# Two score components side by side in a two-bank PSUM tile, and a values product with the queries moving, in a two-layer hybrid encoder

## The chip, the cores and the metric

The kernel runs on one core of a Trainium2 chip. The core has five engines, each with its own queue of instructions: TensorE (PE, with its weight loads shown as PEld), VectorE (DVE), ScalarE (ACT), GpSimd (POOL) and SyncE (SP), which issues the DMAs here. They share an on-chip memory of 128 partitions (SBUF); TensorE writes its results into PSUM, which has eight banks of 512 float32 per partition. The metric is the device time of one execution in microseconds, the median of several runs; lower is better.

## The reference

Two layers of a bidirectional encoder on 512 tokens of width 1024, in float32. Each layer projects the normed input to two groups of heads, puts their outputs through one output projection, and ends in a gated feed-forward with a short convolution. The change concerns the scores of both groups and the values and norm of group B:

```python
def one_block(qi):                      # group B: differential attention
    s = jnp.einsum('bqhcd,bkhcd->bhcqk', qi, k) * scale      # c: two components of 64
    p = jax.nn.softmax(s, axis=-1)
    w = p[:, :, 0] - lam * p[:, :, 1]
    return jnp.einsum('bhqk,bkhd->bqhd', w, v)               # v: 128 wide
...
ya = windowed_gqa_sink(qa, ka, va, sink[l])                  # group A: 8 heads of 64, window of 3 blocks
yb = diff_attention(qb, kb, vb, lam)                         # group B: 4 heads
yb = rmsnorm(yb, subln[l]) * (1.0 - lambda_init)
y = jnp.concatenate([ya, yb], axis=-1)
x = x + y @ w_out[l]
h = rmsnorm(x, g_ffn[l])
gate, val = jnp.split(h @ w_up[l], 2, axis=-1)
x = x + (silu(dwconv(gate)) * val) @ w_down[l]
```

## The kernel before

**Numbers.** Every product is made with float32r operands split into a high and a low part, as three matmuls (`mm3`, lines 193 to 196: high by high, high by low, low by high). `split_out` (line 245) makes the two parts: ScalarE rounds, VectorE subtracts.

**Stages.** The residual lies transposed in SBUF, as eight tiles of 128 features by 512 tokens. Weights come from DRAM in units of up to 512 KB, issued by SP, and are split by ScalarE (line 181) and VectorE or POOL (line 182), three units ahead of their use. In each layer come the input projection (`project`, 24 matmuls with 256 moving columns per block of 128 tokens), the attention of group A and group B, the output projection (`out_pass`, `out_tail`, `out_last`), the norm, and the feed-forward (`up` and `dn`).

**Order.** `weave` (line 121) mixes two tracks of program order by the costs that each step yields: `attend()`, with a total of ATT = 92, and the track of projections for group B and of most of the output projection, with a total of 98.6. A step that yields a function waits until that holds. `out_last(1)`, the second half of the last pass of the output projection, runs behind the weave. From the program order the framework builds a list per engine with its own model of time, in which an instruction that is ready may go ahead of an earlier one that isn't; a tile is taken from its pool when its first writer is placed, and given back behind its last reader.

**PSUM.** Eight banks: two of tag `mm` (projections), four single banks of tag `at` (scores and transposes), one `acc` (sums over many products), one `tq` (small transposes).

**Group A** (`a_scores`, `a_values`). For each of 2 x 4 pairs of head group and query block, twice: two heads' scores, each with 64 rows of contraction on its own half of the partitions, in two banks. Six matmuls, with 256 or 384 key columns, alternate the two (line 412). The masked maximum, the softmax and a division follow; then each key block is transposed (line 457), split and multiplied with the values.

**Group B** (`b_scores`, `b_values`, `b_norm`). For each half (two heads), query block `qb` and head `j`: six matmuls of 512 key columns for components 0 and 1 (line 502), two maxima (line 505), two exps that also sum (line 509), the difference of the weights (line 517). Two units later (LAG = 2): four transposes of the weights (line 529), the split, and 12 matmuls with the transposed weights stationary and 128 value columns moving (lines 538 to 541), so that queries lie on partitions. Per query block and half `b_norm` copies, squares, sums along the row (line 556), takes the root on POOL (`rsqrt`, line 243), scales (line 562), transposes back (line 566) and splits (lines 575 and 576).

Of the kernel before, what the change touches and what calls it, by code (L numbers as in the profile page):

```python
# [34 lines left out]
YP = 3  # L35
# [8 lines left out]
def kernel(  # L44
# [32 lines left out]
    def prob(name):  # L77
        return sb.tile([P, S], F32R, tag="prob", bufs=6, name=name)

    def tmp(name, n=S):  # L80
        return sb.tile([P, n], F32, tag="tmp", bufs=7, name=name)
# [3 lines left out]

    def yp(name):
        return sb.tile([P, CW], F32, tag="yp", bufs=YP, name=name)

# [9 lines left out]
    def at(name):  # L98
        return ps.tile([P, S], F32, tag="at", bufs=4, name=name)
# [9 lines left out]
    def wide(name):  # L109
        cyc["i"] += 1  # L110
        return (mm, at, at)[cyc["i"] % 3](name)
# [155 lines left out]
    for l in range(depth):  # L267
        lam_init = 0.8 - 0.6 * math.exp(-0.3 * l)
# [98 lines left out]
        # group A keys and values, then queries  # L367
# [10 lines left out]
        run(project("akv", akv_done, at))  # L378
# [9 lines left out]
        banks = iter((mm, mm, at, at, at, at, mm, mm))  # L388
# [10 lines left out]
        def a_scores(ip, qb):  # L399
# [7 lines left out]
            for i in range(2):  # L407
                sc = [at(f"sc_{nm}_{i}_{g}") for g in range(2)]
# [36 lines left out]
        def a_values(ip, qb):  # L445
# [6 lines left out]
            for b in range(nkb):  # L452
                tr = at(f"pt_{nm}_{b}")
                for g in range(2):
                    for i in range(2):
                        o = (2 * g + i) * P
                        nc.tensor.transpose(tr[:, o:o + P], so[2 * i + g][:, b * P:(b + 1) * P], ident)
                ph = prob(f"ph_{nm}_{b}")
                pl = prob(f"pl_{nm}_{b}")
                split_out(ph, pl, tr)  # L460
                pb.append((ph, pl))
                yield 0.5
# [25 lines left out]
        def b_scores(half, qb, j):  # L488
            h = 2 * half + j
            if j == 0:  # L490
                b_st[half, qb] = small(f"bl{l}_{half}_{qb}", 4)
            lsum = b_st[half, qb]
# [5 lines left out]
            sc = [at(f"sc_{nm}_{c}") for c in range(2)]  # L498
# [5 lines left out]
            for c in range(2):  # L504
                nc.vector.tensor_reduce(out=mx[:, c:c + 1], in_=sc[c], axis=AX, op=ALU.max)  # L505
            nc.vector.scalar_tensor_tensor(out=mx, in0=mx, scalar=-1.0, in1=rq, op0=ALU.mult, op1=ALU.mult)  # L506
            for c in range(2):
                e.append(tmp(f"e_{nm}_{c}"))
                nc.scalar.activation(e[c], sc[c], AF.Exp, bias=mx[:, c:c + 1], scale=rq[:, c:c + 1],  # L509
                                     accum_out=lsum[:, 2 * j + c:2 * j + c + 1])  # L510
                yield 0.65
            rl = small(f"rl_{nm}", 1)
            nc.vector.reciprocal(rl, lsum[:, 2 * j + 1:2 * j + 2])
            al = small(f"al_{nm}", 1)
            nc.vector.tensor_scalar(out=al, in0=lsum[:, 2 * j:2 * j + 1], scalar1=rl, scalar2=nlam,
# [4 lines left out]
        def b_values(half, qb, j):  # L520
            h = 2 * half + j
            nm = f"b{l}_{h}_{qb}"
            if j == 0:
                b_st[half, qb, "acc"] = accum(f"yb{l}_{half}_{qb}")
            yb = b_st[half, qb, "acc"]
            w = b_st.pop((half, qb, j))
            tr = (mm if half and j else at)(f"wt_{nm}")
            for b in range(NT):
                nc.tensor.transpose(tr[:, b * P:(b + 1) * P], w[:, b * P:(b + 1) * P], ident)
            wh, wl = prob(f"wth_{nm}"), prob(f"wtl_{nm}")  # L530
            split_out(wh, wl, tr)
            yield 0.5
            for first in (True, False):
                for b in range(NT):
                    vh, vl = (v[:, b % 2 * CW + j * P:b % 2 * CW + j * P + P] for v in vb[half, b // 2])
                    o = slice(b * P, (b + 1) * P)
                    if first:
                        nc.tensor.matmul(yb[:, j * P:(j + 1) * P], lhsT=wh[:, o], rhs=vh, start=b == 0, stop=False)
                        nc.tensor.matmul(yb[:, j * P:(j + 1) * P], lhsT=wh[:, o], rhs=vl, start=False, stop=False)
                    else:  # L540
                        nc.tensor.matmul(yb[:, j * P:(j + 1) * P], lhsT=wl[:, o], rhs=vh, start=False, stop=b == NT - 1)
            yield 1.3

        def b_norm(half, qb):
            nm = f"yb{l}_{half}_{qb}"
            yb = b_st.pop((half, qb, "acc"))[:, :2 * P]
            lsum = b_st.pop((half, qb)).rearrange("p (t c) -> p t c", c=2)[:, :, 0]
            le = small(f"le_{nm}", 2)
            nc.vector.scalar_tensor_tensor(out=le, in0=lsum, scalar=EPS / (1.0 - lam_init) ** 2, in1=lsum,
                                           op0=ALU.mult, op1=ALU.mult)  # L550
            y = yp(f"y_{nm}")
            nc.scalar.copy(y, yb)
            sq = yp(f"sq_{nm}")
            nc.scalar.activation(sq, y, AF.Square)
            ss = small(f"ss_{nm}", 2)
            nc.vector.tensor_reduce(out=ss, in_=sq.rearrange("p (t d) -> p t d", d=P), axis=AX, op=ALU.add)
            g2 = (1.0 - lam_init) ** 2
            nc.vector.scalar_tensor_tensor(out=ss, in0=ss, scalar=1.0 / (P * g2), in1=le, op0=ALU.mult, op1=ALU.add)
            rr = small(f"rr_{nm}", 2)
            rsqrt(rr, ss)  # L560
# [19 lines left out]
        def attend():  # L580
# [4 lines left out]
            def values():  # L585
# [5 lines left out]
                else:  # L591
                    yield from b_values(kind, qb, j)
                    while norms:
                        yield from norms.pop(0)
# [201 lines left out]
```

## Time and profile before

| what | value |
|---|---|
| median of 3 runs | 1309.32 us (1308.12 to 1310.32) |
| span of the profiled execution | 1302.4 us |
| mean granted TensorE clock | 0.991 |
| instructions in the profile | 17571 |
| attention, layer 0, from the first scores of A to the last values of B | about 55 to 285 us |
| attention, layer 1 | about 697 to 923 us |
| DMA | 102.96 MB, mean 79 GB/s |

The profile is of one execution; its span runs from the first to the last instruction of the program and is 6.9 us shorter than the median of the runs. "Busy" time of TensorE runs to the modelled end of each matmul and overlaps with the next one, so the distance between two starts tells better what a matmul takes.

### The profile page before, as it was taken

How to read it: one execution, taken by the hardware profiler on the slowest of the kernel's cores; microseconds unless marked ns; L12 is line 12 of the kernel's file. 1: busy time of each engine (PE TensorE's matmuls, PEld its weight loads, DVE VectorE, ACT ScalarE, POOL GpSimd, SP SyncE). 2: the span in 40 equal slices, each digit the busy share in tenths (PEclk: the TensorE clock that was granted, in tenths of full speed). 3: DMA queues.
4: the chain of work that ended last, by engine and by line, in shares of the span. 5: the costliest groups of instructions: out<-in, count | busy, mean ns of one | idle time of the engine just before them, and what ended most of it. 6: DMA issues, size and time to landing. Idle time of an engine off the chain costs nothing. (4 is left out here: it accounts for less than half of the span.)

```text
span 1302.4 us, 17571 instructions
## 1 busy us (share of the span) xinstructions
PE 1270.6 (98%) x6744; PEld 1056.6 (81%) x6744; DVE 772.9 (59%) x1425; ACT 557.5 (43%) x1027; POOL 385.4 (30%) x446
## 2 busy tenths in 40 slices
PE   6999899999999999999999999999899999999998
PEld 6988788687888888888899878877788888888887
DVE  7678787767655324554466786767765543355532
ACT  4566555435433223333455656544443332233321
POOL 6847376114211000110156654741411110011100
PEclk8999999999999999999999999999999999999999
DMA  5211112113332233332331211111133322433232
GB/s 181 91 33 49 58 33 65 33 33 97 98 97 85 85 106 97 98 97 79 100 98 66 65 33 33 56 59 33 33 113 97 97 81 94 117 98 98 79 106 90
DMA packets 32628, 102.96 MB, mean 79 GB/s; under 512 B 3616, under 2 KB 4000, under 8 KB 32544
## 3 DMA queue, kind: packets, MB, share of 16 engines
q1 hardware_dynamic: 32544, 101.84, 25.6%
q8 instruction: 53, 0.87, 0.3%
q14 instruction: 31, 0.25, 0.1%
HBM read 99.73 MB, written 2.10 MB: 78 GB/s over the span
## 5 line engine op out<-in xcount | busy, mean ns | idle before, releaser
L181 ACT CAST wh<-wr 128x1024 fp32r<-128x1024 f32 (+3 forms) x210 | 197.7, 944 | 400.1 <-PE up L195 192.0
L195 PE MATMUL up<-nf_l,wh 128*128 128x512 f32 x704 | 275.3, 391 | 2.3 <-DVE nf_l L213 1.9
L196 PE MATMUL up<-nf_h,wl 128*128 128x512 f32 x704 | 274.5, 390 | 1.2 <-DVE wl L182 0.9
L194 PE MATMUL up<-nf_h,wh 128*128 128x512 f32 x704 | 272.9, 390 | 0.0
L182 DVE TENSOR_TENSOR wl<-wr,wh 128x1024 fp32r<-128x1024 f32 (+3 forms) x174 | 193.3, 1114 | 112.2 <-ACT wh L181 111.8
L702 POOL TENSOR_TENSOR cv<-cv,rb 128x512 f32<-128x512 f32 x44 | 57.8, 1316 | 521.5 <-ACT cv L701 521.5
L195 PEld LDWEIGHTS up<-nf_l,wh 128*128 128x128 f32 x704 | 132.1, 188 | 33.6 <-DVE nf_l L213 6.6
L196 PEld LDWEIGHTS up<-nf_h,wl 128*128 128x128 f32 x704 | 132.1, 188 | 29.7 <-DVE wl L182 2.9
L194 PEld LDWEIGHTS up<-nf_h,wh 128*128 128x128 f32 x704 | 132.2, 188 | 27.6
L195 PE MATMUL dn<-act,wh 128*128 128x512 f32 x352 | 138.5, 394 | 0.0
L196 PE MATMUL dn<-act,wl 128*128 128x512 f32 x352 | 138.4, 394 | 0.0
L194 PE MATMUL dn<-act,wh 128*128 128x512 f32 x352 | 137.9, 393 | 0.0
L182 POOL TENSOR_TENSOR wl<-wr,wh 128x1024 fp32r<-128x1024 f32 x36 | 87.1, 2421 | 89.4 <-ACT wh L181 89.4
L695 DVE TENSOR_TENSOR gp<-up,rb 128x512 f32<-128x512 f32 x44 | 30.3, 693 | 103.4 <-PE up L196 101.8
L703 DVE TENSOR_TENSOR cv<-cv,up 128x512 f32<-128x512 f32 x44 | 30.2, 687 | 82.6 <-POOL cv L702 73.0
L194 PEld LDWEIGHTS dn<-act,wh 128*128 128x128 f32 x352 | 66.0, 188 | 16.0
L195 PEld LDWEIGHTS dn<-act,wh 128*128 128x128 f32 x352 | 66.0, 187 | 15.7
L196 PEld LDWEIGHTS dn<-act,wl 128*128 128x128 f32 x352 | 66.0, 188 | 15.4
L716 DVE TENSOR_TENSOR x<-x,dn 128x512 f32<-128x512 f32 x32 | 22.0, 689 | 78.4 <-PE dn L196 78.4
L509 ACT ACTIVATE e_b<-sc_b,mx_b,rqb 128x512 f32<-128x512 f32 x64 | 49.2, 774 | 38.6 <-DVE mx_b L506 38.6
L701 ACT ACTIVATE cv<-cv 128x512 f32<-128x512 f32 x44 | 27.8, 632 | 76.4 <-DVE cv L700 76.3
L505 DVE TENSOR_REDUCE mx_b<-sc_b 128x1 f32<-128x512 f32 x64 | 42.0, 681 | 0.2
(211 smaller groups left out, 2713.7 us busy)
## 6 DMA issues: line engine op xcount, KB each, us to landing
wr<-w_up SPq DMA_DIRECT2D x88, 512.0 KB, 3.6
wr<-w_in SPq DMA_DIRECT2D x36, 512.0 KB, 3.7
wr<-w_down SPq DMA_DIRECT2D x32, 384.0 KB, 3.1
wr<-w_down SPq DMA_DIRECT2D x32, 320.0 KB, 2.9
wr<-w_out SPq DMA_DIRECT2D x16, 512.0 KB, 3.6
x<-xT SPq DMA_DIRECT2D x8, 256.0 KB, 5.3
outT<-x SPq DMA_DIRECT2D x8, 256.0 KB, 2.0
rows<-row_par SPq DMA_DIRECT2D x2, 260.0 KB, 5.0
```

The costliest lines, as they stand in the source:

```text
L181: nc.scalar.copy(hi[:, o], raw[:, o])
L182: eng.tensor_tensor(out=lo[:, o], in0=raw[:, o], in1=hi[:, o], op=ALU.subtract)
L194: nc.tensor.matmul(acc, lhsT=a[0], rhs=b[0], start=start, stop=False)
L195: nc.tensor.matmul(acc, lhsT=a[0], rhs=b[1], start=False, stop=False)
L196: nc.tensor.matmul(acc, lhsT=a[1], rhs=b[0], start=False, stop=stop)
L505: nc.vector.tensor_reduce(out=mx[:, c:c + 1], in_=sc[c], axis=AX, op=ALU.max)
L509: nc.scalar.activation(e[c], sc[c], AF.Exp, bias=mx[:, c:c + 1], scale=rq[:, c:c + 1], accum_out=lsum[:, 2 * j + c:2 * j + c + 1])
L695: nc.vector.tensor_tensor(out=g[:, 1:S + 1], in0=acc[0], in1=rb, op=ALU.mult)
L701: nc.scalar.activation(cv, cv, AF.Silu)
L702: nc.gpsimd.tensor_tensor(out=cv, in0=cv, in1=rb, op=ALU.mult)
L703: nc.vector.tensor_tensor(out=cv, in0=cv, in1=acc[1], op=ALU.mult)
L716: nc.vector.tensor_tensor(out=x_sb[d], in0=x_sb[d], in1=acc, op=ALU.add)
```

## The change

Scores get a tile of two banks, `at2` (two such tiles in place of four single banks); group A's two heads and group B's two components each take one whole tile. `both` gives its two halves, `wide2` and `halves` hand out pairs of banks to the stages that took single ones. Group A's transposes take one half of such a tile, the `tq` bank or an `mm` bank, by key block. The two maxima of group B become one instruction over both banks.

In group B the order of units becomes half, pair of query blocks `qp`, head, block in the pair. The transposes and the split (`b_weights`) write 128 of 256 columns per key block; after the second block `b_values` multiplies with the values stationary and 256 queries moving, so that the 128 value features lie on partitions. `b_norm` runs once per pair: the square's sum over partitions is a product with `ones`, the root comes back to all partitions through a product with `ident`, and no transposes are needed at its end. ATT and LAG keep their values. Pool sizes change: `prob` from six single to four double tiles, `tmp` from 7 to 8, the rotary tables from four tags of one to one tag of three, and `yp` goes.

```diff
-    def at(name):
-        return ps.tile([P, S], F32, tag="at", bufs=4, name=name)
+    def at2(name):
+        return ps.tile([P, 2, S], F32, tag="at", bufs=2, name=name)
...
-    def wide(name):
+    def wide2(name):
         cyc["i"] += 1
-        return (mm, at, at)[cyc["i"] % 3](name)
+        if cyc["i"] % 3 == 0:
+            return mm(f"{name}a"), mm(f"{name}b")
+        t = at2(name)
+        return t[:, 0], t[:, 1]
+
+    def halves(pick):
+        have = []
+
+        def alloc(name):
+            if not have:
+                have.extend(pick(name))
+            return have.pop(0)
+        return alloc
+
+    def both(name):
+        t = at2(name)
+        return t[:, 0], t[:, 1]
...
-                tabs[i] = sb.tile([P, 2, NT, HD], F32, tag=f"tab{i}", bufs=1, name=f"tab{l}_{i}")
+                tabs[i] = sb.tile([P, 2, NT, HD], F32, tag="tab", bufs=3, name=f"tab{l}_{i}")
...
-        run(project("akv", akv_done, at))
+        run(project("akv", akv_done, halves(both)))
...
-                sc = [at(f"sc_{nm}_{i}_{g}") for g in range(2)]
+                sc = both(f"sc_{nm}_{i}")
...
-                tr = at(f"pt_{nm}_{b}")
+                tr = mm(f"pt_{nm}_{b}") if b == 2 else both(f"pt_{nm}_{b}")[0] if b == 0 else tq(f"pt_{nm}_{b}")
...
-            sc = [at(f"sc_{nm}_{c}") for c in range(2)]
+            sc2 = at2(f"sc_{nm}")
+            sc = (sc2[:, 0], sc2[:, 1])
             for i, (u, v) in enumerate(((0, 0), (0, 1), (1, 0))):
                 for c in range(2):
                     rs = slice(c * HD, (c + 1) * HD)
                     nc.tensor.matmul(sc[c], lhsT=q[u][rs, j, qb * P:(qb + 1) * P], rhs=k[v][rs, j, :],
                                      start=i == 0, stop=i == 2)
-            for c in range(2):
-                nc.vector.tensor_reduce(out=mx[:, c:c + 1], in_=sc[c], axis=AX, op=ALU.max)
+            nc.vector.tensor_reduce(out=mx, in_=sc2, axis=AX, op=ALU.max)
...
+        def b_weights(half, qb, j):
...
+            tr = (mm(f"wt_b{l}_{h}_{qb}") if half and j else both(f"wt_b{l}_{h}_{qb}")[0])
             for b in range(NT):
                 nc.tensor.transpose(tr[:, b * P:(b + 1) * P], w[:, b * P:(b + 1) * P], ident)
-            wh, wl = prob(f"wth_{nm}"), prob(f"wtl_{nm}")
-            split_out(wh, wl, tr)
+            o = slice(qb % 2 * P, qb % 2 * P + P)
+            split_out(wt[0][:, :, o], wt[1][:, :, o], tr.rearrange("p (b q) -> p b q", b=NT))
             yield 0.5
-            for first in (True, False):
-                for b in range(NT):
...
-            yield 1.3
+        def b_values(half, qp, j):
...
+            for b in range(NT):
+                vh, vl = (v[:, b % 2 * CW + j * P:b % 2 * CW + j * P + P] for v in vb[half, b // 2])
+                mm3(yb, (vh, vl), (wt[0][:, b], wt[1][:, b]), b == 0, b == NT - 1)
+                if b % 2:
+                    yield 0.7
+
+        def b_norm(half, qp):
...
+            nc.scalar.activation(y, yb, AF.Copy, scale=cols[:, l, c3:c3 + 1])
+            sq = tmp(f"sq_{nm}")
+            nc.scalar.activation(sq, yb, AF.Square)
...
+            yield 0.2
+            ss = tq(f"ss_{nm}")
+            for i in range(4):
+                nc.tensor.matmul(ss[:, i:i + 1], lhsT=sq[:, i * P:(i + 1) * P], rhs=ones, start=True, stop=True)
+            rr = small(f"rr_{nm}", 4)
+            nc.vector.scalar_tensor_tensor(out=rr, in0=ss[:, :4], scalar=1.0 / (P * (1.0 - lam_init) ** 2), in1=le,
+                                           op0=ALU.mult, op1=ALU.add)
+            rsqrt(rr, rr)
+            yield 0.5
+            rt = tq(f"rt_{nm}")
+            for i in range(4):
+                nc.tensor.matmul(rt[:, i * P:(i + 1) * P], lhsT=rr[:, i:i + 1].broadcast_to([P, P]), rhs=ident,
+                                 start=True, stop=True)
+            nc.vector.tensor_tensor(out=y, in0=y, in1=rt, op=ALU.mult)
...
+            split_out(yh, yl, y.rearrange("p (j q) -> p j q", j=2))
+            b_st["yb", half, qp] = True
+            yield 0.5
...
-            seq += [(half, qb, j) for half in range(2) for qb in range(NT) for j in range(2)]
+            seq += [(half, 2 * qp + i, j) for half in range(2) for qp in range(2) for j in range(2) for i in range(2)]
...
+                yield from b_weights(kind, qb, j)
+                if norms:
+                    yield from norms.pop(0)
+                if qb % 2:
+                    yield from b_values(kind, qb // 2, j)
+                    if j:
+                        g = b_norm(kind, qb // 2)
+                        yield next(g)
+                        norms.append(g)
...
-        run(out_last(1, w_last, wide))
+        run(out_last(1, w_last, halves(wide2)))
...
-                acc = []
+                acc = wide2(f"up{l}_{f}")
                 for j in range(2):
                     w = next_unit()
-                    a = wide(f"up{l}_{f}_{j}")
                     for k in range(NK):
-                        mm3(a, (w[0][:, k, :], w[1][:, k, :]), (h.hi[k], h.lo[k]), k == 0, k == NK - 1)
-                    acc.append(a)
+                        mm3(acc[j], (w[0][:, k, :], w[1][:, k, :]), (h.hi[k], h.lo[k]), k == 0, k == NK - 1)
...
+            wide = halves(wide2)
```

More of the change, by code (lines that the diff above doesn't have):

```diff
@@ L34 @@
 RP = 7
-YP = 3
 SMP = 12
@@ L387 @@
         qk = {}
-        banks = iter((mm, mm, at, at, at, at, mm, mm))
+        pairs_at = halves(both)
+        banks = iter((mm, mm, pairs_at, pairs_at, pairs_at, pairs_at, mm, mm))
         run(proj_a(0, lambda name: next(banks)(name)))
@@ L550, in b_norm @@
                                            op0=ALU.mult, op1=ALU.mult)
[L551 to L558, printed above, removed]
@@ L590, in values @@
                         b_st["ya"] = True
[L591 to L594, printed above, removed]
-                    if j == 1:
-                        norms.append(b_norm(kind, qb))
-                        yield next(norms[0])
+                    return
+                yield from b_weights(kind, qb, j)
[7 more added lines that the diff above has]
+                        norms.append(g)
             for kind, qb, j in seq:
```

81 lines of the change are left out of this document (30 added, 51 removed).

## The prediction

> **What bounds the kernel now.** I read the engine table of the page first, then the busy time of the four attention stretches (two per layer), then what TensorE waits for.
>
> ```profile
> PE 1270.6 (98%) x6744; PEld 1056.6 (81%) x6744; DVE 772.9 (59%) x1425; ACT 557.5 (43%) x1027; POOL 385.4 (30%) x446
> ```
>
> ```profile
> 55.00:150.00 95.00, 93.45 (x644) 80.21 (x645) 74.87 (x209) 57.86 (x147) 55.70 (x53) 0.98 0.15 47
> 150.00:285.00 135.00, 129.28 (x775) 102.94 (x774) 100.83 (x222) 67.70 (x153) 61.48 (x62) 1.00 0.16 48
> 697.00:790.00 93.00, 90.78 (x620) 77.23 (x616) 71.03 (x207) 55.16 (x140) 47.07 (x45) 0.98 0.16 46
> 790.00:923.00 133.00, 130.01 (x798) 106.41 (x798) 94.52 (x218) 69.06 (x156) 59.41 (x51) 0.99 0.16 48
> ```
>
> Columns of these four rows: stretch, its length, busy PE, PEld, DVE, ACT, POOL, then granted clock. The four stretches are 456 us long; TensorE is busy for 443.5 of them, VectorE for 341.3 (75%).
>
> ```profile
> PE pj_akv L194 <- ACT wh L181: 6.2, 1, 6.2
> ...
> PE tr_yb L566 <- DVE y_yb L562: 2.3, 2, 1.1
> PE yb L541 <- DVE wtl_b L247: 1.9, 2, 1.2
> PE up L195 <- DVE nf_l L213: 1.9, 2, 1.0
> ...
> PE na_ss L233 <- DVE na_sum L227: 0.2, 1, 0.2
> ```
>
> These are the first, the last and three of the sixteen rows of what TensorE waited for; all sixteen sum to 26.8 us, and those of attention to about 13.5. So **TensorE's own work sets the time**, in the order in which its queue holds it, and an edit is worth what it takes from TensorE. "Busy" says little of that work, as matmuls overlap in the pipeline; I price by the distance from one start to the next.
>
> **Scores.** Both components of a head contract over 64 rows, one on partitions 0 to 63, the other on 64 to 127. The first fence has two rows of the group view (behind the bar: busy us as a union, mean ns of one), the next three the order of time (start, length, count).
>
> ```profile
> L502 PE MATMUL sc_b<-bkh,bqh 64*128 64x512 f32 x64 | 27.9, 490 | 0.0
> L412 PE MATMUL sc_a<-ka,qal 64*128 64x256 f32 (+1 forms) x64 | 16.5, 318 | 0.0
> ```
>
> ```profile
> 227.76 0.41 PE L566 MATMUL tr_yb<-ident,y_yb 128*128 128x128 f32 x2
> 228.10 0.50 PE L502 MATMUL sc_b<-bkh,bqh 64*128 64x512 f32 x1
> ...
> 228.99 0.66 PE L529 MATMUL wt_b<-ident,e_b 128*128 128x128 f32 x4
> ```
>
> ```profile
> 882.65 0.50 PE L502 MATMUL sc_b<-bkh,bqh 64*128 64x512 f32 x2
> ...
> 883.54 0.50 PE L194 MATMUL wo<-yh,wh 128*128 128x512 f32 x1
> ```
>
> ```profile
> 102.64 0.50 PE L412 MATMUL sc_a<-ka,qah 64*128 64x256 f32 x4
> ...
> 103.19 0.38 PE L194 MATMUL pj_bk<-wh,na_h 128*128 128x256 f32 x1
> ```
>
> ```profile
> 122.24 0.28 PE L194 MATMUL pj_bk<-wh,na_h 128*128 128x256 f32 x1
> 122.36 0.28 PE L195 MATMUL pj_bk<-wl,na_h 128*128 128x256 f32 x1
> 122.57 0.62 PE L412 MATMUL sc_a<-ka,qah 64*128 64x384 f32 x4
> ...
> 123.30 0.38 PE L196 MATMUL pj_bk<-wh,na_l 128*128 128x256 f32 x1
> ```
>
> At 228.10 one component's three matmuls stand alone and take 0.89 us until the next work. At 882.65 both components' six (rows of x2: pairs with one start) take 0.89 us too. So **a pair costs what one costs**, if its two halves stand next to each other. How many do? In the row of L502, 64 times 490 ns is 31.4 us, the union is 27.9; the missing 3.5 us is 7 overlapping pairs of 32, so 25 heads run apart. L412's row in the same way: 64 x 318 ns = 20.4, less 16.5, is 3.9 us or 12 pairs, so 20 of 32 apart. Before the change each component had its own bank, and the queue took the first as soon as one bank was free. Afterwards one allocation gives both banks, so all six become ready together and their program order alternates the components.
>
> A run that is saved saves its entry as well: before 122.57 the distance is 0.21 where two projections are 0.12 apart, so 0.09. Group B: 25 x (0.89 + 0.09) = **-24.5 us**. Group A: six take 0.73 us at 384 columns and 0.55 at 256 (rows 122.57 and 102.64), half of the blocks each, so 20 x (0.64 + 0.09) = **-14.6**. Bounds: nothing, if the queue still puts other work between the components, and -39.1; the rows with x2 and x4 show that what is ready together stays together, so I take it whole.
>
> **Values product turned round.**
>
> ```profile
> 272.03 0.31 PE L538 MATMUL yb<-vb,wth_b 128*128 128x128 f32 x1
> ...
> 272.96 0.61 PE L541 MATMUL yb<-vb,wtl_b 128*128 128x128 f32 x4
> 273.40 0.45 PE L649 MATMUL wo<-yh_b,wh 128*128 128x256 f32 x2
> ```
>
> Twelve matmuls with 128 moving columns take 272.03 to 273.40, 1.37 us or 0.114 each; with 256 columns the distance is 0.12 (122.24 to 122.36). Before: 32 units of 12, 43.8 us. After: 16 units of 12 at 0.12, 23.0 us. **-20.8**. The transposes of the weights (L529) stay 128 in number, and their split keeps its size.
>
> [...]
>
> **Norm over partitions.** The nearest rows are the same forms in the layer norm: four one-column products (8 passes) and four broadcasts against ident (8 passes), from the chain view.
>
> ```profile
> 948.89 0.79 PE nf_ss L233 x8
> 956.19 0.89 PE rps L673 x8
> ```
>
> Eight norms at 0.79 + 0.89, with two entries of 0.09, add 14.9 us. Sixteen pairs of transposes (L566) go, 0.34 us each from 227.76 to 228.10: -5.4. Net **+9.5**.
>
> **Sum on TensorE**: -24.5 - 14.6 - 20.8 + 9.5 = -50.4 us.
>
> **The end of each attention.**
>
> ```profile
> 282.75 0.40 PE L649 MATMUL wo<-yl_b,wh 128*128 128x256 f32 x2
> 284.28 0.41 PE L566 MATMUL tr_yb<-ident,y_yb 128*128 128x128 f32 x2 [1.13 <-DVE y_yb L562]
> 285.25 0.50 PE L649 MATMUL wo<-yh_b,wh 128*128 128x256 f32 x2 [0.56 <-ACT yh_b L575]
> 285.60:288.80 3.20, 3.20 (x21) 3.20 (x20) 0.11 (x1) 0.00 (x0) 0.00 (x0) 0.63 0.02 5
> ```
>
> The last norm is bare: from 282.75 + 0.24 to 285.25 TensorE does only two transposes (0.24), so 2.0 us are lost, and the clock then reads 0.63 for 3.2 us. The new chain is longer: two ACT passes, ss, a sum, rsqrt on POOL, broadcast, product, cast; with 0.79 and 0.89 for the two matmul steps and 0.685 for the product on VectorE (rows above and below), and five more steps taken as of that order, some 6 to 7 us, an estimate. But the costs that attend() yields fall: group A's stay 39.0, group B's go from 16 x 3.1 + 8 x 0.35 = 52.4 to 16 x 1.8 + 8 x 1.4 + 4 x 1.2 = 44.8. ATT stays 92, so attend() ends when 91% of the other track's 98.6 is out, and about 9 us of output projection are left over to cover the chain. I take both gaps as gone, -4.0, and 0.5 us per layer of the slow clock (1.2 us by the row, but the VectorE chain behind it, the wait of up on nf_l, is late next and keeps most): **-5**.
>
> **Off the path.**
>
> ```profile
> L505 DVE TENSOR_REDUCE mx_b<-sc_b 128x1 f32<-128x512 f32 x64 | 42.0, 681 | 0.2
> L562 DVE TENSOR_TENSOR y_yb<-y_yb,rr_yb 128x256 f32<-128x256 f32 x16 | 9.9, 618 | 2.7 <-POOL rr_yb L243 2.4
> L247 DVE TENSOR_TENSOR act<-cv,act 128x512 fp32r<-128x512 f32 x44 | 30.2, 685 | 1.4 <-ACT act L246 1.4
> ```
>
> VectorE's 64 maxima become 32 of twice the length (between 0.68 and 1.36 us each; I take 1.2, near the upper end, as the length doubles: 42.0 to 38.4). The norm's 16 products of 256 columns become 8 of 512 at 0.685, 9.9 to 5.5, its other steps also halve in number, and one reduction goes. All of that is hidden behind TensorE and worth nothing by itself; with at least 8 us gone, VectorE has at most 333 us in a stretch of some 401, 83% where it was 75%. The new scale and square on ACT read 512 columns where they read 256, half as often: ACT is far from its bound (249.8 us of 456). The fourth rotary table now waits on POOL for one of three buffers, until group A's keys are done; its first reader, bk0, stands four chunks of projection later in the program, so nothing. No DMA is moved, added or taken away.
>
> **New waits.** Each norm now makes VectorE wait for TensorE twice (rr behind ss, the product behind rt), with the next unit's maximum queued behind it; its exps and, through them, its score slot wait for that. And the score slots become two of two banks, which the transposes also take while using half. One unit's hold:
>
> ```profile
> L502 PE MATMUL sc_b<-bkh,bqh x32: 393/493/501, 148.9 to 268.7; 64*128 64x512 f32 x32
> 231.47 0.68 DVE L247 TENSOR_TENSOR wtl_b<-wt_b,wth_b 128x512 fp32r<-128x512 f32 x1
> 233.02 0.77 ACT L509 ACTIVATE e_b<-sc_b,mx_b,rqb 128x512 f32<-128x512 f32 x1
> ```
>
> Scores at 228.10 are released at 233.8 (5.7 us), transposes at 228.99 at 232.2 (3.2 us): 8.9 us on two slots per unit. Sixteen units in 148.9 to 268.7 are 7.5 us each, some 6.3 afterwards: 12.6 us of slots. That fits at 71%, and projection matmuls fill. Bounds of the added waits: 0, as the queue has other work, to 25 us, if all sixteen norm waits cost the longest tr_yb wait (1.1) and attention's other waits (10 us) nearly double. I take **+8**, nearer to the rows of waits, which are small.
>
> **Total**: the profiled execution's span is 1302.4; -50.4 - 5 + 8 gives 1255.0. The runs' median of 1309.3 is 6.9 us above that span, so **1262 us**, 3.6% faster.
>
> **Rivals.** (1) *The cover gets thin*: VectorE's share and the shared PSUM tiles (tq is now also taken by group A's second block) bring 25 us of waits or more: 1280. For it: up to 83% on VectorE; against: 13.5 us of waits today. (2) *The components still run apart*, since the queue puts other work between: -20.8 + 9.5 - 5 + 4 from 1309, 1297. Against it: the x2 and x4 rows. [...] (4) *Slower*: a scores group can't start until both exps of the one before have left their two-bank slot, and TensorE's in-order queue stands behind it. There are 64 groups; it decides from 0.75 us of bare wait per group (47 us in all); at 1.1 us it gives 1332. Against: slots at 71%, and no wait for a score bank among the sixteen rows.
>
> **How the numbers follow.** Forecast 0.70 (1243 with no added waits, whole clock gain and fewer changes of form, to 1275), rival 1 0.14, rival 2 0.07, rival 3 0.03, rival 4 0.05; 0.01 for no change. Range 1243 to 1288: it leaves out rivals 2 and 4 and some of rival 1 and of my own case. A measurement of this kernel tells 0.2% from no change, 2.6 us: faster 0.94, same 0.01, slower 0.05.
>
> **What would show it.** Rows of L502 and L412 with x2 and x4, and a union of sc_b near 32 x 0.5 for the first product; half as many yb matmuls at 0.12; ss and rt with eight passes near 0.8 to 0.9 us; no bare wait ahead of the last output projection; attention near 205 us per layer where it was 228. Wrong if score runs of three remain, if TensorE's waits list names sc_b or wt_b with more than 20 us, or if VectorE passes 90% there.

## The result, and the profile after

| | median | range | runs |
|---|---|---|---|
| before | 1309.75 us | 1308.12 to 1310.32 | 4 |
| after | 1350.82 us | 1349.14 to 1352.15 | 4 |

The ratio is 1.0315 with a 95% interval of 1.030 to 1.033: the changed kernel is 3.2% slower, where 1262 us and 3.6% faster were forecast. The profiled execution has a span of 1348.4 us, 46.0 more than before.

Where the time went is read from the view of windows, cut at the borders of the stages: first projection, attention of layer 0 (from its first score to its last output projection), feed-forward, and the same for layer 1. First the kernel before; the columns are stretch, length, busy PE, PEld, DVE, ACT, POOL, granted clock, DMA share, GB/s.

```profile
0.00:55.30 55.30, 43.68 (x310) 41.84 (x310) 38.12 (x70) 27.68 (x58) 39.24 (x51) 0.94 0.43 141
55.30:292.50 237.20, 229.98 (x1466) 190.41 (x1467) 178.64 (x438) 127.46 (x302) 116.88 (x114) 0.99 0.15 46
292.50:660.30 367.80, 366.05 (x1604) 298.57 (x1603) 185.48 (x220) 133.15 (x174) 51.79 (x80) 1.00 0.32 95
660.30:696.60 36.30, 36.30 (x305) 36.19 (x303) 23.23 (x56) 19.72 (x42) 27.27 (x32) 1.00 0.27 88
696.60:930.70 234.10, 228.38 (x1464) 191.21 (x1464) 168.83 (x433) 126.96 (x299) 106.62 (x97) 0.98 0.15 46
930.70:1302.40 371.70, 366.23 (x1603) 298.42 (x1601) 178.61 (x212) 122.50 (x157) 43.59 (x74) 1.00 0.31 95
```

The same view of the changed kernel:

```profile
0.00:60.60 60.60, 47.20 (x312) 44.63 (x312) 38.01 (x70) 26.75 (x56) 40.32 (x51) 0.89 0.39 128
60.60:309.80 249.20, 220.00 (x1426) 187.32 (x1426) 177.66 (x402) 129.32 (x298) 117.05 (x109) 0.92 0.15 46
309.80:682.40 372.60, 366.17 (x1597) 297.51 (x1596) 179.23 (x216) 129.27 (x167) 48.66 (x79) 1.00 0.30 92
682.40:720.00 37.60, 36.82 (x303) 36.11 (x301) 21.81 (x52) 17.75 (x37) 24.16 (x30) 1.00 0.27 84
720.00:970.40 250.40, 217.17 (x1418) 182.49 (x1418) 171.59 (x399) 126.73 (x294) 112.07 (x99) 0.94 0.14 43
970.40:1348.40 378.00, 368.84 (x1603) 300.05 (x1601) 171.61 (x210) 120.83 (x154) 40.64 (x73) 1.00 0.30 94
```

A row splits into three parts. Length less busy PE is TensorE's **idle** time. Length times (1 - clock) is what the lower **clock** took. What is left is TensorE's **work at full clock**. For both attentions together, before: 471.3 = 12.9 idle + 7.1 clock + 451.3 work. After: 499.6 = 62.4 idle + 35.0 clock + 402.2 work. So the work fell by some 49 us, near the forecast of 50.4, and idle time and clock took 77 back. (The clock has two digits, which makes a sum good to about 2 us. The clock part also counts idle time inside a stretch at half clock, so the work comes out too low where TensorE idles much. Counted by the busy time alone inside the half-clock stretches of the trace, the clock took 8.5 us before and 31.2 after, and the work fell by 44, from 449.9 to 405.8.) The other four stages, in which nothing was to be won or lost, are 17.7 us longer.

The groups of TensorE in the two attentions show the forecast work (behind the bar: busy as a union, mean ns of one; then idle before):

```profile
L516 PE MATMUL sc_b<-bkh,bqh 64*128 64x512 f32 x64 | 17.2, 534 | 4.9 <-DVE p_a L259 2.2 <-DVE wl_b L259 1.2 <-ACT bkh L258 0.9
L206 PE MATMUL yb<-wh_b,vb 128*128 128x256 f32 x64 | 20.2, 315 | 1.4 <-ACT wh_b L258 1.4
L580 PE MATMUL rt_yb<-ident,rr_yb 128*128 128x128 f32 x64 | 8.5, 276 | 0.2 <-POOL rr_yb L255 0.2
L572 PE MATMUL ss_yb<-ones,sq_yb 128*128 128x1 f32 x64 | 8.4, 252 | 0.0
```

64 times 534 ns is 34.2 us, the union is 17.2: nearly all pairs of components now run side by side. Before, 31.4 stood against 27.9. Over all three products the union of group B's scores fell from 54.8 to 36.2 us, and that of group A's from 37.3 to 25.0.

The new products of group B in order of time, near the end of layer 1's attention:

```profile
949.60 0.28 PE L208 MATMUL yb<-wh_b,vb 128*128 128x256 f32 x1
...
950.79 0.39 PE L206 MATMUL wo<-yh_b,wh 128*128 128x512 f32 x1
...
953.60 0.95 PE L572 MATMUL ss_yb<-ones,sq_yb 128*128 128x1 f32 x8
954.41 0.48 PE L206 MATMUL wo<-yh_b,wh 128*128 128x512 f32 x1
...
957.27 1.05 PE L580 MATMUL rt_yb<-ident,rr_yb 128*128 128x128 f32 x8
958.08 0.48 PE L665 MATMUL wo<-yh_b,wh 128*128 128x256 f32 x2
```

The last ten of the twelve values matmuls take 1.19 us, 0.119 each; `ss` and `rt` take 0.81 us each. These are the forecast prices (0.12, 0.79 and 0.89).

What TensorE waits for (us in total, times, longest) has new names at its head:

```profile
PE pt_a L470 <- DVE so_a L454: 12.0, 8, 2.0
PE tr_bk L369 <- DVE bkl L259: 8.1, 6, 2.5
PE pj_bv L206 <- DVE vb L376: 7.7, 4, 2.7
PE pj_akv L206 <- ACT wh L193: 6.6, 1, 6.6
PE pt_a L470 <- DVE bql L259: 5.3, 2, 3.8
```

The scores wait little (4.9 us in the row of L516). What waits are group A's transposes (`pt_a`), the small transposes (`tr_bk`, in `tq`) and projections (`pj_bv`, in `mm`). The first row is a wait for the weights themselves (`so_a`), not for a bank; it was 1.5 us before. The last is a wait for `tq`. Its longest in order of time, from the rows of TensorE, VectorE and POOL:

```profile
771.11 0.28 PE L425 MATMUL sc_a<-ka,qal 64*128 64x256 f32 x2
775.21 0.66 PE L470 MATMUL pt_a<-ident,so_a 128*128 128x128 f32 x4 [3.82 <-DVE bql L259]
...
771.27 3.22 DVE L454 TENSOR_SCALAR so_a<-so_a,rl_a 128x256 f32<-128x256 f32 x4
774.75 0.41 DVE L259 TENSOR_TENSOR bql<-tr_bq,bqh 128x256 fp32r<-128x256 f32 x1
...
771.84 2.51 POOL L194 TENSOR_TENSOR wl<-wr,wh 128x1024 fp32r<-128x1024 f32 x1 [2.09 <-ACT wh L193]
```

The second key block of group A is to be transposed into `tq`. That bank holds `tr_bq`, and its last reader, `bql`, stands on VectorE behind four scalings of group A's softmax, one of which takes 2.43 us beside POOL's subtraction of 2.51 us. TensorE stands still for 3.82 us, although the weights to be transposed had been scaled by 763.43; the four scalings are the next unit's. Before the change these transposes went to whichever of four score banks was free, and none of them waited for `tq`.

More idle time came with a lower clock. Four neighbouring stretches of 3.41 us around the wait of `pj_bv` for `vb`, same columns as above:

```profile
151.09:154.50 3.41, 2.20 (x18) 1.29 (x14) 1.89 (x7) 2.52 (x9) 0.00 (x0) 1.00 0.00 0
154.50:157.92 3.42, 1.34 (x11) 1.34 (x12) 2.18 (x7) 2.25 (x7) 0.00 (x0) 1.00 0.02 5
157.92:161.33 3.41, 3.41 (x17) 3.31 (x17) 0.90 (x3) 0.33 (x1) 0.00 (x0) 0.51 0.00 0
161.33:164.74 3.41, 3.41 (x29) 3.27 (x28) 3.15 (x12) 1.22 (x3) 0.00 (x0) 0.99 0.00 0
```

TensorE idles for 1.21 and then 2.08 us; the next 3.41 us, from 157.99 to 161.40 in the trace, are granted half the clock, with 17 matmuls where the stretch behind has 29. At 0.51 of the clock these 3.41 us cost 1.7 us, on top of the 3.3 us of idle time. In both attentions together 49.5 us more idle time came with 28 us more clock.

### The profile page after: what moved, and what is told of

Read it like the earlier page. It is cut to its first block, busy times and chain, and to the rows that moved or that the text cites. A ratio compares the mean times of both kernels' runs of the same rounds, so it can differ in the third digit from the quotient of the medians.

```text
span 1348.4 us, 17285 instructions
## 1 busy us (share of the span) xinstructions
PE 1256.2 (93%) x6648; PEld 1048.1 (78%) x6648; DVE 759.9 (56%) x1345; ACT 550.7 (41%) x1003; POOL 382.9 (28%) x438
## 4 chain that ended last, share of the span: by engine, by line
PE 75%; DVE 12%; ACT 5%; issue 4%; POOL 3%; DMA 1%; SPq 0%; POOLq 0%; ACTq 0%; DVEq 0%
PE up L207 8%; PE up L208 8%; PE up L206 8%; PE dn L207 4%; PE dn L206 4%; PE dn L208 4%; ACT so_a L447 2%; DVE so_a L454 2%; PE wo L206 1%; PE wo L207 1%; PE wo L208 1%; PE sc_b L516 1%; DVE so_a L429 1%; ACT wh L193 1%; PE wt_b L542 1%
## 5 line engine op out<-in xcount | busy, mean ns | idle before, releaser
L207 PE MATMUL up<-nf_l,wh 128*128 128x512 f32 x464 | 180.9, 390 | 1.0 <-DVE nf_l L225 1.0
L206 PE MATMUL up<-nf_h,wh 128*128 128x512 f32 x464 | 180.6, 389 | 0.0
L208 PE MATMUL up<-nf_h,wl 128*128 128x512 f32 x464 | 180.5, 389 | 0.0
L207 PEld LDWEIGHTS up<-nf_l,wh 128*128 128x128 f32 x464 | 87.1, 188 | 19.7 <-DVE nf_l L225 1.9
L206 PE MATMUL dn<-act,wh 128*128 128x512 f32 x240 | 96.1, 400 | 6.4 <-ACT wh L193 3.5
L206 PEld LDWEIGHTS up<-nf_h,wh 128*128 128x128 f32 x464 | 87.1, 188 | 18.1
L208 PEld LDWEIGHTS up<-nf_h,wl 128*128 128x128 f32 x464 | 87.1, 188 | 17.8
L207 PE MATMUL dn<-act,wh 128*128 128x512 f32 x240 | 95.9, 400 | 0.4 <-DVE act L259 0.4
L208 PE MATMUL dn<-act,wl 128*128 128x512 f32 x240 | 94.9, 398 | 0.0
L206 PEld LDWEIGHTS dn<-act,wh 128*128 128x128 f32 x240 | 45.4, 189 | 20.9 <-ACT wh L193 4.3
L207 PEld LDWEIGHTS dn<-act,wh 128*128 128x128 f32 x240 | 45.8, 191 | 11.9 <-DVE act L259 1.1
L206 PE MATMUL pj_bv<-wh,na_h 128*128 128x256 f32 x128 | 41.0, 320 | 7.7 <-DVE vb L376 7.7
```

The lines of the kernel that those rows point to most:

```text
L206: nc.tensor.matmul(acc, lhsT=a[0], rhs=b[0], start=start, stop=False)
L207: nc.tensor.matmul(acc, lhsT=a[0], rhs=b[1], start=False, stop=False)
L208: nc.tensor.matmul(acc, lhsT=a[1], rhs=b[0], start=False, stop=stop)
```

## The experiments

The first theories were **P**: the PSUM part costs the time (two-bank slots, and `tq` and `mm` shared with group A's transposes); **V**: the turned values product and the norm cost it; **C**: what TensorE saves comes back as idle time and lower clock in any case.

**1. Values and norm alone**, in four single score banks.

```diff
-    def at2(name): ... [P, 2, S], tag="at", bufs=2
+    def at(name): ... [P, S], tag="at", bufs=4
-                sc = both(f"sc_{nm}_{i}")
+                sc = [at(f"sc_{nm}_{i}_{g}") for g in range(2)]
-  tr = mm(...) if b == 2 else both(...)[0] if b == 0 else tq(...)
+  tr = at(f"pt_{nm}_{b}")
```

> Values product turned round and norm over partitions alone; scores, transposes and feed-forward in four single banks as before. Theory P (the PSUM part of the change, two-bank slots and the shared tq and mm banks, costs the time): faster than before by 11 to 20 us (-20.8 + 9.5 on TensorE, and the gap at the end), 1290 to 1299. Theory V (the turned values and the longer norm chain cost the time, by waits of TensorE): slower than before, 1330 or more. Theory C (TensorE's own work fell, and what fills its waits fell with it, whichever part goes): between, 1300 to 1315.

1305.97 us, ratio 1.000 (0.998 to 1.002). The part is worth nothing, and it does no harm: V falls. The time lies in C's range, not in P's. In its attentions the work is 21 us less, and idle time and clock together are 28 more.

**2. The two-bank part alone**, values and norm as before.

```diff
-            sc = [at(f"sc_{nm}_{c}") for c in range(2)]
+            sc2 = at2(f"sc_{nm}")
+            sc = (sc2[:, 0], sc2[:, 1])
```

> Two-bank score tiles and the sharing of tq and mm alone; values, norm and order of units in group B as before. Theory P: slower than before by as much as the change or more, 1350 to 1370, with TensorE waiting for pt_a, tr_bk and projections. Theory V: faster than before, 1270 to 1290. Theory C: 1310 to 1340.

1351.22, ratio 1.035 (1.030 to 1.039). This part alone gives the whole loss, and its work is nevertheless some 34 us less (29 by the busy time alone). For this part P holds.

**3. The changed kernel, group A's transposes out of `tq` and `mm`**, two key blocks in the halves of a two-bank tile.

```diff
-  tr = mm(...) if b == 2 else both(...)[0] if b == 0 else tq(...)
+  tr = pick(f"pt_{nm}_{b}")       # pick = halves(both)
```

> The changed kernel, but group A's transposes take the halves of two-bank tiles (two key blocks in one tile, the third in another), and neither tq nor mm. If the sharing of tq and mm is what costs within theory P: 1310 to 1330, and the waits of pt_a for bql and of tr_bk go. If the two slots themselves are: 1350 or more.

1339.22, ratio 1.026 (1.021 to 1.030): 12 us back, between the two ranges. `pt_a` no longer stands in the list of waits, and `tr_bk` waits 1.8 us for `bkl`. Its attentions:

```profile
61.20:311.00 249.80, 220.94 (x1426) 187.16 (x1426) 176.80 (x402) 130.20 (x298) 116.35 (x109) 0.92 0.15 46
721.20:963.80 242.60, 220.50 (x1418) 185.86 (x1418) 168.88 (x399) 127.69 (x293) 110.65 (x99) 0.91 0.14 44
```

With that sharing gone they still take 492.4 us, where the changed kernel's take 499.6 and those of the kernel before 471.3.

**4. The changed kernel, ATT 84.**

```diff
-ATT = 92.0
+ATT = 84.0
```

> The changed kernel with ATT = 84, about the sum of the costs that attend() now yields, so that both tracks end together as before. If the time is lost since attention runs ahead of the work that fills its waits: faster by 5 to 20 us, 1330 to 1345. If the waits come from slots: within 5 us of 1351, and the end of the attention waits for its last norm again.

1343.21, ratio 1.029 (1.025 to 1.033): 8 us back, in the range of the first case.

**5. Side by side without two-bank tiles.** The kernel before, and only an order on TensorE's queue, so that five of a unit's six matmuls alternate the halves.

```diff
+            for m in range(2, 6):
+                behind(ms[m], ms[m - 1])     # order only, no semaphore
```

> The kernel before, with its four single score banks, and only an order added: within a unit of scores each matmul from the third on stands behind the one before it, so that five of the six alternate the halves; values, norm, transposes as before. Theory P (the loss is the price of two-bank slots and of shared tq and mm; side by side is worth its TensorE time): a unit falls from two runs (1.96 us) to one matmul and a run of five (about 1.2), some 22 heads of B x 0.7 and some 15 of A x 0.6, -24 us: 1283 to 1292. Theory E (what TensorE saves in attention is eaten, as the softmax chains set the pace): 1306 to 1312, with TensorE's idle and half-clock time up by about what was saved.

1290.96, ratio 0.987 (0.985 to 0.989). The idea of the change is good; its banks are not. Work is 20 us less, idle time nearly the same (12.3), clock 11 more. But with five of six in order only part of the overlap is there: the union of group B's scores is 46.8 us (54.8 before, 36.2 in the changed kernel), that of group A's 32.6 (37.3 and 25.0).

**6. Values, norm and ordered scores**, single banks: experiment 1 with the lines of 5.

```diff
+            for m in range(2, 6):
+                behind(ms[m], ms[m - 1])     # in a_scores and b_scores
```

> The values product turned and the norm over partitions (the run of these alone), single banks, with the same added order of the scores. Theory P: the saving of the order on top of that run's 1306: 1275 to 1290. Theory E: 1303 to 1312, and half-clock time above the 48 us of that run's two attentions.

1291.84, ratio 0.987 (0.986 to 0.989): as fast as 5, no faster, and just above P's range. This is the base for what follows: the changed kernel without its PSUM part, with the order of 5 in place of the two-bank tiles.

**7. Experiments 3 and 4 together.**

```diff
-ATT = 92.0
+ATT = 84.0
...
+  tr = pick(f"pt_{nm}_{b}")
```

> The changed kernel with both cures at once: group A's transposes in halves of two-bank tiles (alone: 1339) and ATT 84 (alone: 1343). If the two cure different waits (theory P): 1329 to 1334. If they cure the same idle time (theory E): 1336 to 1342.

1343.33, ratio 1.028 (1.025 to 1.031). The two cures don't add: the time is that of 4 alone and lies above both ranges. What they do to each other isn't shown.

**8. One score bank less**, in the kernel before.

```diff
-        return ps.tile([P, S], F32, tag="at", bufs=4, name=name)
+        return ps.tile([P, S], F32, tag="at", bufs=3, name=name)
```

> The kernel before with three single score banks in place of four, nothing else. Theory P (TensorE's queue lives on the banks it can run ahead into): 1320 to 1345, with longer TensorE idle in attention. Theory E (banks are not what the chains wait for): 1306 to 1313.

1335.62, ratio 1.021 (1.019 to 1.024). One bank is worth 27 us to this kernel, as P had it. One row of its waits, which had 1.5 us in the kernel before:

```profile
PE pt_a L457 <- DVE so_a L441: 7.6, 5, 2.3
```

**9. Base 6, with the sharing of the changed kernel.**

```diff
-                tr = at(f"pt_{nm}_{b}")
+                tr = (at, tq, mm)[b](f"pt_{nm}_{b}")
```

> The kernel of values, norm and ordered scores in single banks (1292), and group A's transposes go, as in the changed kernel, by key block to a score bank, the tq bank and an mm bank. If sharing tq and mm with the projections is a price of its own (theory P; its removal from the changed kernel gave 12 us): 1300 to 1310. If it hurt only because the two-bank slots had made everything late (rival): 1289 to 1296, since a score bank is free in its place.

1331.63, ratio 1.020 (1.016 to 1.024): 40 us for one line, although it takes work off the score banks; both ranges were far too low. Its attentions, then those of base 6:

```profile
53.70:305.80 252.10, 228.03 (x1418) 189.67 (x1418) 170.04 (x417) 125.48 (x292) 118.03 (x109) 0.91 0.15 44
707.40:955.40 248.00, 222.03 (x1417) 184.78 (x1416) 164.68 (x409) 123.28 (x288) 107.44 (x96) 0.94 0.15 43
```

```profile
53.40:284.50 231.10, 218.90 (x1418) 180.80 (x1418) 170.88 (x417) 125.89 (x292) 117.36 (x109) 0.96 0.16 48
686.10:916.50 230.40, 218.04 (x1416) 180.49 (x1416) 166.33 (x409) 123.57 (x288) 108.90 (x96) 0.97 0.16 47
```

500.1 us against 461.5, with 25.4 more idle and 21.4 more clock. The changed kernel's attentions take 499.6. So in attention this sharing alone is enough for a loss of the changed kernel's size. It isn't the only way to it: experiment 3 has none of it, and its attentions are 31 us longer than those of base 6.

**10 and 12. Base 6 with ATT 84 and 98.**

```diff
-ATT = 92.0
+ATT = 84.0     # 10
+ATT = 98.0     # 12
```

> The same kernel of 1292 us with ATT 84 in place of 92, about what the fall of the costs that attend() yields amounts to. If the weave is out of step (theory): 1280 to 1288. If the bare waits are chains of one unit, which no mix changes: 1290 to 1296.

> The same kernel of 1292 us with ATT 98, the other way. If the weave is out of step towards 84: 1294 to 1302. If chains of one unit set the waits: 1289 to 1296. If lower than 1288, the attention track was too far ahead and not too far behind.

1310.45 and 1310.17, ratios 1.003 (1.001 to 1.005) and 1.002 (1.000 to 1.004): 18 us more on either side. 92 fits here too, and neither expectation was right. No bank changes hands in these two, so they also tell how much another order of the same work can cost base 6.

**11. Base 6, the transposed weights holding a second bank** that they don't need.

```diff
+            spare = at(f"spare_b{l}_{h}_{qb}")
+            nc.tensor.transpose(spare[:, :P], w[:, :P], ident)
...
+            nc.vector.tensor_tensor(out=wt[1][...][:, :1], in0=spare[:, :1], in1=..., op=ALU.subtract)
```

> The same kernel of 1292 us; group B's transposed weights take a second score bank with them, where the changed kernel takes a two-bank tile and uses half: a fifth transpose writes it and one VectorE instruction of one column reads it behind the split, so it is held as long. [...] Theory P (the half-used bank is a large part of the price; one bank less throughout cost 27): 1302 to 1318. Rival (it is the pair that has to come free at once, or the sharing): 1291 to 1298.

1296.47, ratio 0.993 (0.990 to 0.995): 4.6 us, of which some 2.7 are the 24 added transposes, an estimate at the 0.114 us that a matmul of 128 columns takes in row 272.03 of the kernel before. In base 6 the half-used tile is not the price.

**13 and 14. Base 6, sharing only `tq`, only `mm`.**

```diff
-                tr = at(f"pt_{nm}_{b}")
+                tr = (at, tq, at)[b](f"pt_{nm}_{b}")     # 13
+                tr = (at, at, mm)[b](f"pt_{nm}_{b}")     # 14
```

> The kernel of 1292 us (values, norm, ordered scores, single banks); of group A's transposes only the second key block goes elsewhere, to the one tq bank. In the run that shared both banks tr_bk waited 6.1 us and pt_a 3.7 behind the small transposes' split, most of it through tq. If tq is the price: 1318 to 1332. If mm is: 1292 to 1302. If the two add up: 1305 to 1318.

> The same kernel; only the third key block (half of the units have one) goes to one of the two mm banks. If mm, where the projections need both banks, is the price: 1318 to 1332. If tq is: 1292 to 1302. If the two add up: 1305 to 1318.

1317.08 and 1302.99, ratios 1.008 (1.005 to 1.011) and 0.998 (0.996 to 1.000): 25 and 11 us, together 36 of the 40. The numbers fit two prices that add up, with `tq` the larger, but 11 lies below the 18 us of experiments 10 and 12 and 25 not far above: neither is shown for itself.

**15. Order for group B's scores alone**: experiment 5 without its lines in `a_scores`.

```diff
-                for m in range(2, 6):          # a_scores
-                    behind(ms[m], ms[m - 1])
```

> The kernel before with the added order for group B's scores alone. With both groups ordered it took 1291, 17 us less. By TensorE's work B is worth 22 x 0.7 = 15 and A 15 x 0.6 = 9, so if what is saved is lost evenly: 1296 to 1300. If A's side by side is worth nothing because group A waits for its softmax: 1290 to 1294. If B's is worth nothing: 1304 to 1310.

1299.21, ratio 0.994 (0.992 to 0.996): B gives 8 us; with A's order too (5) it is 17 to 18.

**16. The changed kernel, sums of the down projection in order.**

```diff
+                    if k == 0 and end is not None:
+                        behind(m[0], end)
```

> The changed kernel, with an order added in the feed-forward alone: each sum of the down projection stands behind the end of the one before it in TensorE's queue. In the changed kernel two matmuls of the next pair stand ahead of the pair's second half and wait for weights not yet split (0.69 us at 487.97). If that is what makes the two feed-forwards 5 and 6 us longer: 1341 to 1347, the stages 372.6 and 373.4 back near 368. If the stages wait for weights for another reason: 1348 to 1353.

1358.07, ratio 1.036 (1.032 to 1.041), and the feed-forwards stay long (374.8 and 377.7 us, where the changed kernel has 372.6 and 378.0). The expectation failed, but the wait it uncovered names a cause. The row of this run, then that of the changed kernel:

```profile
PE dn L211 <- DVE x L740: 8.4, 10, 0.9
```

```profile
PE dn L206 <- DVE x L731: 1.7, 2, 0.9
```

Ten waits of 0.84 us for the addition of a sum to the residual; in order of time each stands between the two sums of one pair. There are 16 pairs of sums, and two in three lie in a two-bank tile: about ten. So the second half of a tile waits until its first half is read, though it is another bank; in the changed kernel two matmuls of the next pair stand between, which wait for their weights instead (0.69 us at 487.97).

**17. The changed kernel, first projection in four tiles.**

```diff
-        run(project("akv", akv_done, halves(both)))
+        akv_banks = iter((mm, mm, lambda n: both(n)[0], lambda n: both(n)[0]))
+        run(project("akv", akv_done, lambda name: next(akv_banks)(name)))
```

> The changed kernel, with the first projection's four token blocks in four tiles (two mm banks and one half of each two-bank tile) in place of two tiles' four halves. In the changed kernel 48 of its 96 matmuls are out by 24 us and none more until 32 us, as if the second half of a tile had to wait for the first; before, 74 are out by 24 us. If a tile's matmuls keep their program order and this makes the first stage 5 us longer: 1343 to 1348, with about 74 out by 24 us. If the stage is late for another reason: 1349 to 1353.

1351.05, ratio 1.033 (1.029 to 1.036): unchanged as a whole. But the mechanism is there. The windows of the changed kernel and of this run:

```profile
20.00:30.00 10.00, 9.63 (x41) 8.96 (x42) 6.24 (x12) 1.01 (x4) 4.23 (x5) 0.50 0.34 107
```

```profile
20.00:30.00 10.00, 9.88 (x72) 9.68 (x72) 7.03 (x12) 2.36 (x4) 3.79 (x4) 0.86 0.30 102
```

In the changed kernel the first halves' 48 products end at 24 us, and the second halves wait for the first to be read, which needs the norm. In four tiles the first stage takes 54.0 us instead of 60.6 and that of layer 1 33.5 instead of 37.6. The attentions, whose code is the same, became 14 us longer.

**18. Base 6, the norm's two products in a score bank**, not in `tq`.

```diff
-            ss = tq(f"ss_{nm}")
+            ss = at(f"ss_{nm}")
-            rt = tq(f"rt_{nm}")
+            rt = at(f"rt_{nm}")
```

> The kernel of 1292 us (values, norm, ordered scores, single banks), with the norm's two small products in a score bank and not in the tq bank. Sharing tq with group A's transposes cost 25 us. If the norm's use of tq is what eats the turned values product's saving (with and without it: 1292 and 1291): 1278 to 1287. If not: 1289 to 1297.

1307.08, ratio 0.999 (0.997 to 1.001): 15 us more, above both ranges. It takes a score bank, and 15 us lie within what another order alone costs (10 and 12), so it doesn't tell what the tie on `tq` is worth.

The three parts of the length of both attentions, worked out from the windows as above:

| kernel | length | idle | clock | work |
|---|---|---|---|---|
| before | 471.3 | 12.9 | 7.1 | 451.3 |
| after | 499.6 | 62.4 | 35.0 | 402.2 |
| 1 values and norm | 477.9 | 23.6 | 23.9 | 430.4 |
| 2 two-bank part | 500.8 | 56.2 | 27.5 | 417.1 |
| 3 sharing out | 492.4 | 51.0 | 41.8 | 399.6 |
| 5 ordered scores | 462.5 | 12.3 | 18.5 | 431.7 |
| 6 base | 461.5 | 24.6 | 16.2 | 420.8 |
| 8 one bank less | 504.3 | 20.4 | 27.8 | 456.1 |
| 9 base, shared | 500.1 | 50.0 | 37.6 | 412.5 |
| 10 base, ATT 84 | 476.2 | 36.0 | 23.8 | 416.4 |
| 12 base, ATT 98 | 485.0 | 33.4 | 34.0 | 417.6 |
| 13 `tq` only | 484.4 | 37.1 | 31.5 | 415.8 |
| 14 `mm` only | 474.4 | 34.5 | 23.8 | 416.1 |

The rows of 6, 9, 10, 12, 13 and 14 have the same matmuls, and their work differs by up to 8.3 us: that is how far the split can be trusted.

## Why the prediction was wrong

**The bound** was read rightly for the kernel before: TensorE's work. It isn't the bound of the changed kernel, whose TensorE idles for 62 of 500 us.

**Scores, -24.5 and -14.6**: right in mechanism, and near as work. Experiment 2 has 29 to 34 us less than before, of 39.1 forecast. Ordered in single banks both groups give 17 to 18 us of time, about half each; that is with less than half of the overlap, so what all of it would be worth in time isn't shown.

**Values -20.8, norm +9.5**: right in sign and mechanism. Experiment 1 has 17 to 21 us less work where 11 were forecast; the rows of `yb`, `ss` and `rt` above have the forecast prices, so what the rest is stays open. The chance of 0.03 for rival 3 was for 256 columns at twice the cost of 128; no run shows that: they took 0.119 us a matmul, where 128 took 0.114 before. As time the part is worth nothing (experiment 1, and 6 against 5). Whether its norm's use of `tq` is the reason isn't shown (18), and the cause stays open.

**End of attention, -5**: the gap is gone; no wait of the last output projection for `yh_b` is left in the list (in layer 1 it waits 0.5 us for `x`), and `rt` waits 0.2 us. The clock it was to spare was lost many times over elsewhere.

**Off the path**: the double maximum was costed at 1.2 us and measures 1.216. VectorE is no bound: 349 of 500 us, 70%, not 83%. But its busy time didn't fall by 8 us as forecast. It does in experiment 1 (347.5 to 339.8 us); in experiment 2 it grows by 14. "The shared PSUM tiles" stand in the forecast only as part of rival 1.

**New waits, +8, bounds 0 to 25: this is the step that failed.** In its place the runs show 49.5 us more idle time and 28 us of clock in attention, and they come from the PSUM part (2 against 1). The slots were reckoned for group B's scores and transposed weights alone ("fits at 71%"); in base 6 the half-used tile indeed costs next to nothing (11). What the sum left out is that group A's transposes go to `tq` and `mm`, banks that other chains use. That alone costs base 6 40 us (9). In size it is enough for attention's loss, but it isn't the only price: with two-bank slots and group A's transposes out of `tq` and `mm` (3) the attentions are still 31 us longer than in base 6. The two prices don't add up, and which of them sets the changed kernel's time stays open. The bound of 25 was taken from the waits of a kernel that had spare banks; with one bank less the same kernel loses 27 us (8). And a wait was priced at its own length, without the clock that went with it, 28 us here.

**The other stages**, costed at nothing: 17.7 us. The prediction has no term for what `halves` does. A write to the second half of a tile waits for the read of the first where the program has them in that order: ten waits of 0.84 us in 16, and 41 matmuls from 20 to 30 us in the changed kernel (at 0.50 of the clock) where 17, with four tiles, has 72 (at 0.86). That this is all of the 17.7 us isn't shown.

**Rivals.** Rival 4 has the right sign by the wrong mechanism: score groups wait for a slot, 0.75 us at 64 places. They wait 4.9 us in the row of L516. Rival 1 names the shared tiles, `tq` among them, and so one of the mechanisms, and puts 25 us or more and 1280 to it. With -55 us on the other side, waits had to reach 55 us to turn the sign; they reached 77, and 18 more came from outside. None of the signs named in advance as proof of error appeared (scores' waits over 20 us, VectorE over 90%, score runs of three), so they were the wrong ones to watch.

**What is not settled.** An edit changes the planner's order everywhere: 16 touches only the feed-forward, and its attentions are 13 us longer; 17 likewise. Base 6 with another ATT, and nothing else, is 18 us slower (10 and 12). A difference of 10 to 18 us from one kernel is therefore not one cause. The 40 and the 27 us lie well above that; the 25 of 13 doesn't by much. The 17 us of 5 and 6 don't lie above it, but 5, 6 and 15 all fall the same way, and the overlap is in their rows. The removals from the changed kernel (3, 4, 7: 12, 8 and 7 us) are smaller than the 40 us that the sharing costs base 6. A reason may be that group A's transposes then take two-bank slots, whose second half waits for the first; no run tests it.

The fastest kernels are 5 and 6, some 17 us under the kernel before.

## What to carry to other kernels

Price a change of PSUM by asking for each bank who else uses it, and what stands on the queue of its last reader; a short list of waits in a kernel with spare banks says little of what it costs to lose them (27 us for one bank in 8). New waits of a TensorE that was bound by its work cost more than their length in these runs: 49.5 us more idle time came with 28 us of clock, 25.4 with 21.4 in 9 against 6, and 7.5 with 21 in 8 against the kernel before. If two products are only to stand side by side, order them in the queue and leave the banks single; that gave the fastest kernels here.

## What the runs showed of the hardware that was not expected

**The clock.** The trace of the changed kernel has 14 stretches at half clock inside its span, 3.41 to 20.48 us long. In the 3.41 us before each, TensorE was idle for 1.35 to 2.97 us by the trace, and its longest single gap was 0.76 to 2.82 us: half clock followed gaps that short.

**VectorE beside POOL.** Six of the scalings of `so_a` took 2.35 to 2.52 us in the changed kernel, each with POOL's subtraction beside it for 2.2 us or more; without it most take 0.34 to 0.42. The kernel before has seven such (1.91 to 2.65 us). There TensorE waited 1.5 us in all for `so_a`, with one score bank less 7.6 (8), after the change 12.0: the stall is old, and the spare banks seem to have hidden it.
